# Scores of two attentions as three products of split queries and keys, and raw weights in pieces

## The chip, the cores and the metric

The kernel runs on one core of one Trainium2 chip. The metric is the device time of one execution in microseconds (us), lower is better; three runs of the kernel before gave 2064.75, 2060.04 and 2063.96, and their median, 2063.96, is the time before.

## The reference

Two transformer-like blocks on 256 tokens of width 1024, each two layers deep, all in float32. What matters here is where scores are formed:

```python
# first block, per layer: three branches on h = rms_norm(x)
y_a = mamba2_branch(...)                 # chunked state-space scan
y_b = sliding_window_branch(...)         # "banded": 16 heads of 64, 4 key heads, window 128, rope, sinks
#   scores = einsum('bnqkgd,bnskd->bnkgqs', qb, kb) * HEAD_DIM ** -0.5
y_c = forgetting_attention_branch(...)   # 16 heads, causal, decay by cumulated gates, no rope
x = x + sum(sigmoid(gate_i) * (y_i @ w_proj_i)) @ w_out

# second block, per layer: tokens x and a context of 256 tokens, 8 heads, 2 key heads
q, k = apply_rope(q), apply_rope(k)      # the tokens' own, not the context's
s_lat = einsum('bnqhgd,bnkhd->bhgnqk', qb, kb) * scale     # blocks of 128, neighbours within 128
s_ctx = einsum('bnqhgd,bchd->bhgnqc', qb, kc) * scale      # 256 context keys
o = softmax([s_lat, s_ctx, sink]) @ [v, vc]
# in layer 0 the context attends to itself as well; then pool, fourier, merge, conv_ffn
```

## The kernel before

The width lies on the 128 partitions, 8 chunks of it, with the 256 tokens along the free axis (512 in the second block's first layer, where tokens and context run together).

**Dense products.** Every weight matrix is multiplied in three products of split operands (`mm3`): high part by high part, high by low, low by high. The parts are of type fp32r, a form of float32 that TensorE takes in one pass. A unit of weights is a [128, 2048] tile. `fetch` loads it raw as one DMA of 1 MB on SyncE's queue (tile `wr`), then in four pieces of 512 ScalarE copies the high part (`wh`, recorded at line L98) and VectorE, or GpSimd for one of the pieces, subtracts to get the low part (`wl`, L101). The three tiles each have 3 buffers, so the loads run about two units ahead. Only the first units, for which a callback `between` is given, come in four DMAs.

**Scores.** The attentions multiply plain float32: `qk` (L234) forms the scores of two heads, which stand on partitions 0 to 63 and 64 to 127, for the banded and the forgetting branch; the inner function `score` of `attention` does so in the second block, with 512 keys in two halves of 256. Queries and keys are turned by `rope`: four small DMAs swap halves into a second tile, GpSimd and VectorE multiply, VectorE adds (tiles `f` from a ring of 13, later 10 buffers; `swk` for the banded keys, `kv` for the second block's keys and values).

**Order.** The order of TensorE's instructions is the order in which the code issues them: a running count of rows gives a `tick` each 3072 rows (`spent`), and a tick advances the waiting tasks (rope, weights) and the attention jobs, each in three steps (scores; transposes of the probabilities; values). So the attention's small pieces stand at fixed places among the dense products. The other engines' instructions are put in order by a scheduler at build time. Pools with a fixed number of buffers decide who waits for whom.

All TensorE work is recorded at L92 (matmul) and L95 (transpose), ScalarE's at L98, VectorE's at L101 and L104, since helpers issue it: the groups are told apart by their tiles. `pd` is the PSUM tile of dense products, `ps` of scores, `pt` of transposes, `po` of values.

Of the kernel before, what the change touches and what calls it, by code (L numbers as in the profile page):

```python
# [6 lines left out]
F32 = mybir.dt.float32  # L7
F32R = mybir.dt.float32r
# [3 lines left out]
ALU = mybir.AluOpType  # L12
# [33 lines left out]
class Kern:  # L46
    def __init__(self, ctx, tc, A, out, dbg=None):
        self.tc, self.nc, self.A, self.out = tc, tc.nc, A, out
        self.dbg = dbg or {}
        nc = tc.nc  # L50
        self.V, self.S, self.P, self.T = nc.vector, nc.scalar, nc.gpsimd, nc.tensor
        p = lambda name, bufs, **kw: ctx.enter_context(tc.tile_pool(name=name, bufs=bufs, **kw))
        self.cst_p = p("cst", 1)
        self.w_p = p("w", 3)
        self.wl_p = p("wlo", 3)
        self.x_p = p("x", 1)
        self.m_p = p("wm", 2)
        self.r_p = p("r", 3)
        self.sm_p = p("sm", 2)
        self.dram_p = p("dram", 1, space=bass.MemoryType.DRAM)  # L60
        self.ps_d = p("psd", 3, space=PSUM)
        self.ps_s = p("pss", 2, space=PSUM)
        self.ps_t = p("pst", 2, space=PSUM)
        self.ps_o = p("pso", 1, space=PSUM)
        self.t = self.rows = 0
        self.on_pool = (1024,)
        self.tasks = []
        self.jobs = []
        self.waiting = []
        self.cur = self.nxt = None  # L70
# [44 lines left out]
    def fetch(self, between=None, on_pool=None):  # L115
        ap, kt, ncol = self.queue.pop(0)
        n = kt * ncol
        on_pool = self.on_pool if on_pool is None else on_pool
        raw = self.w_p.tile([128, 2048], F32, name="wr", tag="wr")
        hi = self.w_p.tile([128, 2048], F32R, name="wh", tag="wh")  # L120
        lo = self.wl_p.tile([128, 2048], F32R, name="wl", tag="wl")
        if between is None:
            self.nc.sync.dma_start(raw[:, :n], ap)
        step = 512
        for o in range(0, n, step):
            s = slice(o, o + step)
            if between is not None:
                between(o // step)
                self.nc.sync.dma_start(raw[:, s], ap[:, s])
            self.act(hi[:, s], raw[:, s])  # L130
            self.tt(lo[:, s], raw[:, s], hi[:, s].bitcast(F32), ALU.subtract, self.P if o in on_pool else None)
        v = lambda t: t[:, :n].rearrange("p (k c) -> p k c", k=kt)
        self.ready.append((v(hi), v(lo)))

# [99 lines left out]
    def qk(self, pss, cuts, q, k):  # L234

        for a, b, c, d in cuts:
            for i, ps in enumerate(pss):
                p = slice(64 * i, 64 * i + 64)
                self.mm(ps[:, a:b], q[p, 128 * (a > 0):128 * (a > 0) + 128], k[p, c:d], True, True)

    def masked(self, out, ps, mask, least, init=3e38):

# [267 lines left out]
def b1_layer(K, l, x, yr, sums, cw, wdt, first_sums=None):  # L510
# [210 lines left out]
    for i in range(4):  # L721
# [26 lines left out]
        def score(pair, pss, q=q, kk=kk, i=i):  # L748
            K.qk(pss, ((0, 128, 0, 128), (128, 384, 0, 256)), q[:, pair, :], kk[:, pair, :])
# [22 lines left out]
            K.tt(m, m, th, ALU.add, K.P)  # L772


    def rope(t):
        s = K.f2((128, 2, 256))
        for a in range(4):
            b = a ^ 1
            nc.scalar.dma_start(s[32 * a:32 * a + 32], t[32 * b:32 * b + 32])

        def task():
            yield 2
            K.tt(s, s, K.bc(K.rope[:, 1, :], 2), ALU.mult, K.P)
            K.tt(t, t, K.bc(K.rope[:, 0, :], 2), ALU.mult)
            yield 1
            K.tt(t, t, s, ALU.add)

        turned = K.spawn(task())
        K.step(turned)
        return turned  # L790

    ps = K.dense(K.unit(), H, (0, 1))
    kk = K.k_p.tile([128, 2, 256], F32, name="swk", tag="k0")
    K.act(kk, ps)
    kturned = rope(kk)
    ps = K.dense_tok(K.unit(), H)
    v = K.k_p.tile([128, 2, 256], F32, name="swv", tag="k1")
    K.act(v, ps)
    yb = K.r_p.tile([128, 2, NK, 256], F32R, name="yb", tag="r16")
    nsk = K.small([128, 16], "nsk")  # L800
# [1 line left out]
    for i in range(4):  # L802
        g0 = 2 * (i // 2)
        ps = K.dense(K.unit(), H, (0, 1))
        q = K.f2((128, 2, 256))
        K.act(q, ps, scale=-0.125)
        turned = rope(q)
        zs = gate_z(K.dense(K.unit(), H, (0, 1)))

        def score(pair, pss, q=q, i=i):  # L810
            K.qk(pss, ((0, 128, 0, 128), (128, 384, 0, 256)), q[:, pair, :], kk[:, i // 2, :])

        def fix(pair, i=i):
            s = slice(4 * i + 2 * pair, 4 * i + 2 * pair + 2)
            return (nsk[:, s],
                    vec("sink", 16 * l, 16)[:, s].unsqueeze(2).to_broadcast([128, 2, 2]))

        js = attn4(score, lambda j, t, g0=g0: v[:, t, 64 * (g0 + j % 2):64 * (g0 + j % 2) + 64],
                   (K.msk("u"), K.msk("le", 2)), fix, gated(yb, zs, 2 * i), 2, (turned, kturned))
        jb += js  # L820
        gate_proj(2, yc, i, jc, True)
# [196 lines left out]
def b2_layer(K, l, x, hin, last, after):  # L1018
# [25 lines left out]
    cs64 = c2[:, 3072:3328]  # L1044
    poolw = c2[:, 3328 + 256 * l:3328 + 256 * l + 256].rearrange("p (c d) -> p c d", c=2)

    def rope(t):

        sw = K.f2((128, 256))
        for q in range(4):  # L1050
            b = q ^ 1
            nc.scalar.dma_start(sw[32 * q:32 * q + 32], t[32 * b:32 * b + 32])
        def task():
            yield 2
            K.tt(sw, sw, K.rope2[:, 1, :], ALU.mult, K.P)
            K.tt(t, t, K.rope2[:, 0, :], ALU.mult)
            yield 1
            K.tt(t, t, sw, ALU.add)

        turned = K.spawn(task())  # L1060
        K.step(turned)
        return turned


    kt = K.kv[:, 0:512]
    v = K.kv[:, 512:1024].rearrange("p (t c) -> p t c", t=4)
    yp = r16((128, 2, 4, 512), "yp2", K.rx_p)
    ya = r16((128, 2, 4, 512), "ya2")
# [51 lines left out]

    def keys(s, Hs):
        ps = K.dense(wkv, Hs, (0, 1))
        K.act(kt[:, tok(s)], ps[:, 0, :])
        if s == 0:
            turned_k.append(rope(kt[:, 0:256]))
        vtasks.append(K.spawn(values_task(s, ps[:, 1, :])))

    def pools(s, Hs):
# [95 lines left out]
    def attention(pair, q, turned):  # L1224
        sh, js = {}, []

        def done(o):
            split(ya[:, 0, pair, 0:W], ya[:, 1, pair, 0:W], o)

        for qb in range(2):  # L1230
            def score(pss, qb=qb):
                for a in range(2):
                    for i, ps in enumerate(pss):
                        p = slice(64 * i, 64 * i + 64)
                        K.mm(ps[:, 256 * a:256 * a + 256], q[p, 128 * qb:128 * qb + 128],
                             kt[p, 256 * a:256 * a + 256], True, True)

            js.append(attn_pair(sh, pair, 128 * qb, score, 1, K.msk("lt" if qb else "zero", 4), lambda b, i: v[:, b, 64 * i:64 * i + 64],
                                done if last and qb else None))
        if not last:  # L1240
            def score(pss):
                for qb in range(2):
                    for i, ps in enumerate(pss):
                        p = slice(64 * i, 64 * i + 64)
                        K.mm(ps[:, 256 * qb:256 * qb + 256], q[p, 256 + 128 * qb:384 + 128 * qb], kt[p, 256:512],
                             True, True)

            js.append(attn_pair(sh, pair, 256, score, 2, None, lambda b, i: v[:, 2 + b % 2, 64 * i:64 * i + 64], done))
        return K.enqueue(js, 1, (turned, *keyed))

    ja = []
    for i in range(2):
        w = K.unit(1 if last and i == 0 else 2)
        for job in jobs:
            q = K.f2((128, len(job), W))
            K.act(q, K.dense(w, H, job), scale=-0.125)
            if last and i == 0:
                project(1, (keys,))
            keyed = turned_k + vtasks
            for ci, c in enumerate(job):  # L1260
                turned = rope(q[:, ci, 0:256])
                ja += attention(2 * i + c, q[:, ci, :], turned)

    K.finish(*ptasks)
    merged = K.big_p.tile([128, NK, W], F32, name="merged2", tag="m")
# [303 lines left out]
def program(tc, A, out, dbg=None):  # L1569
    with ExitStack() as ctx:  # L1570
# [14 lines left out]
        with ExitStack() as c1:  # L1585
            p = lambda name, bufs, **kw: c1.enter_context(tc.tile_pool(name=name, bufs=bufs, **kw))
            K.big_p, K.sm1_p, K.k_p = p("big1", 1), p("sm1", 1), p("k1", 1)
            K.f_p = p("f1", 13)
            K.ones = K.cst_p.tile([128, 128], F32, name="ones")
            V.memset(K.ones, 1.0)  # L1590
            warm = K.small([128, 1], "warm")
# [50 lines left out]
            def between(js):  # L1642
                b1_raw(K, 1, x1, yr, js)
                if js.start == 4:
                    wdt.extend(b1_wdt(K, 1))
# [45 lines left out]
        with ExitStack() as c2:  # L1691
# [2 lines left out]
            K.f_p = p("f2", 10)  # L1694
            kv = K.m_p.tile([128, 2048], F32, name="kv", tag="wm")
            K.kv = kv[:, 0:1024]
            K.rope2 = kv[:, 1024:1536].rearrange("p (c n) -> p c n", c=2)
            nc.sync.dma_start(K.rope2, A["rope2"])

# [248 lines left out]
```

## Time and profile before

| | us |
|---|---|
| median of three runs | 2063.96 |
| the profiled execution | 2062.68 |
| its span on the core | 2060.9 |
| TensorE (PE) busy | 2029.2 (98%) |
| VectorE (DVE) busy | 1464.4 (71%) |
| ScalarE (ACT) busy | 991.1 (48%) |
| GpSimd (POOL) busy | 506.2 (25%) |
| mean granted TensorE clock | 0.994 |

PE's matmuls are recorded with overlapping ends, so its busy time counts stretches without a gap: what one product costs is read from the distance between two starts. An instruction that shows an idle time in brackets waited for the instruction behind the arrow. Busy times of the other engines count only where PE waits for them.

### The profile page before, as it was taken

Reading aid. Unit: us, or ns where it says so; the run is one execution under the profiler, and the core shown is the slowest. Engines: PE = TensorE matmul, PEld = TensorE weight load, DVE = VectorE, ACT = ScalarE, POOL = GpSimd, SP = SyncE. Lnnn points to the kernel's source line nnn. Section 1 sums busy time; section 2 is a strip of 40 time slices with the busy share of each in tenths; the row PEclk is TensorE's granted clock in tenths of the full one; section 3 lists DMA queues with packets and bytes.
Section 4 is the critical chain, followed back from the end, with each engine's and each line's share of the span. In section 5 each row is a group of like instructions: output and inputs, shape, how many; then the busy total and the mean of one; then the engine's idle time right before and its main releaser. Section 6 shows DMA issues by size and latency. Waiting matters only on the chain.

```text
span 2060.9 us, 37605 instructions
## 1 busy us (share of the span) xinstructions
PE 2029.2 (98%) x14768; PEld 1839.0 (89%) x14768; DVE 1464.4 (71%) x2835; ACT 991.1 (48%) x2112; POOL 506.2 (25%) x393
## 2 busy tenths in 40 slices
PE   8999999999999999999999999999999999999998
PEld 7898999999898999999877888888888899999997
DVE  7777788976777788978466454865564576879984
ACT  6455555545455555555344333542332354556553
POOL 3232222324333123343100212111111121232222
PEclk9999999999999999999999999999999999999999
DMA  7765656665765656654111232232222233454552
GB/s 272 292 214 191 219 207 248 222 246 203 259 208 195 233 202 243 231 191 162 59 57 57 87 123 102 83 102 94 91 103 92 92 128 118 144 195 164 182 192 77
DMA packets 66304, 339.08 MB, mean 165 GB/s; under 512 B 7760, under 2 KB 22096, under 8 KB 29776
## 3 DMA queue, kind: packets, MB, share of 16 engines
q1 hardware_dynamic: 62000, 332.22, 45.7%
q10 hardware_dynamic: 4128, 4.46, 0.8%
q8 instruction: 116, 1.90, 0.4%
q14 instruction: 60, 0.49, 0.1%
HBM read 331.28 MB, written 1.44 MB: 161 GB/s over the span
## 4 chain that ended last, share of the span: by engine, by line
PE 92%; DVE 5%; issue 1%; ACT 1%; DMA 1%; SPq 0%; POOL 0%; DVEq 0%; POOLq 0%; ACTq 0%
PE pd L92 81%; PE ps L92 4%; PE po L92 3%; PE pt L92 2%; PE pt L95 2%; DVE wl L101 2%; DVE f L104 1%; DVE f L101 1%; ACT wh L98 0%; DMA wm<-in_wm_dram 0%; DVE h L104 0%; DMA x<-in_x_dram 0%; DVE f L984 0%; DVE hl L101 0%; ACT f L98 0%
## 5 line engine op out<-in xcount | busy, mean ns | idle before, releaser
L101 DVE TENSOR_TENSOR wl<-wr,wh 128x512 fp32r<-128x512 f32 x751 | 687.9, 934 | 244.7 <-ACT wh L98 243.1
L98 ACT ACTIVATE wh<-wr 128x512 fp32r<-128x512 f32 x992 | 561.2, 621 | 470.1 <-PE pd L92 262.1
L101 POOL TENSOR_TENSOR wl<-wr,wh 128x512 fp32r<-128x512 f32 x241 | 349.9, 1452 | 1238.9 <-ACT wh L98 1103.0
L92 PE MATMUL pd<-h,wh 128*128 128x256 f32 x2688 | 498.7, 286 | 2.4 <-ACT wh L98 1.4
L92 PEld LDWEIGHTS pd<-h,wh 128*128 128x128 f32 x2688 | 417.5, 191 | 26.4 <-issue 17.6
L92 PE MATMUL pd<-h,wl 128*128 128x256 f32 x1344 | 380.0, 283 | 0.7 <-DVE wl L101 0.7
L92 PE MATMUL pd<-hh,wh 128*128 128x512 f32 (+1 forms) x992 | 347.6, 350 | 1.5 <-ACT hh L98 1.5
L92 PE MATMUL pd<-hl,wh 128*128 128x512 f32 (+1 forms) x992 | 341.4, 344 | 3.7 <-DVE hl L101 3.7
L92 PE MATMUL pd<-hh,wl 128*128 128x512 f32 (+1 forms) x992 | 340.4, 343 | 0.0
L92 PEld LDWEIGHTS pd<-h,wl 128*128 128x128 f32 x1344 | 257.2, 191 | 1.2 <-DVE wl L101 0.9
L92 PEld LDWEIGHTS pd<-hh,wh 128*128 128x128 f32 x992 | 189.9, 191 | 30.4 <-issue 7.5
L92 PEld LDWEIGHTS pd<-hl,wh 128*128 128x128 f32 x992 | 190.1, 192 | 25.5 <-DVE hl L101 4.7
L92 PEld LDWEIGHTS pd<-hh,wl 128*128 128x128 f32 x992 | 190.0, 192 | 21.6
L92 PE MATMUL pd<-act,wh 128*128 128x256 f32 (+1 forms) x688 | 160.2, 327 | 0.0
L104 DVE SCALAR_TENSOR_TENSOR f<-pd,cw,f 128x255 f32<-128x255 f32 (+3 forms) x272 | 151.0, 555 | 11.0 <-ACT f L98 8.6
L92 PEld LDWEIGHTS pd<-act,wh 128*128 128x128 f32 x688 | 116.2, 190 | 11.1 <-DVE act L101 0.2
L92 PE MATMUL pd<-hf,wh 128*128 128x256 f32 x640 | 115.2, 283 | 0.0
L92 PE MATMUL pd<-mg,wh 128*128 128x256 f32 (+1 forms) x576 | 113.0, 296 | 0.1
L92 PE MATMUL pd<-act,wl 128*128 128x256 f32 (+1 forms) x344 | 112.2, 326 | 0.0
L98 ACT ACTIVATE f<-f,mn 128x128 f32<-128x128 f32 (+2 forms) x160 | 79.8, 500 | 46.8 <-DVE mn L243 46.6
L98 ACT ACTIVATE f<-pd,cw 128x256 f32<-128x256 f32 (+1 forms) x120 | 66.8, 557 | 69.6 <-DVE f L104 62.7
L92 PEld LDWEIGHTS pd<-hf,wh 128*128 128x128 f32 x640 | 99.8, 192 | 0.0
(257 smaller groups left out, 3216.5 us busy)
## 6 DMA issues: line engine op xcount, KB each, us to landing
wr<-in_w_dram SPq DMA_DIRECT2D x233, 1024.0 KB, 4.9
wm<-in_wm_dram SPq DMA_DIRECT2D x48, 1024.0 KB, 6.9
f<-far SPq DMA_DIRECT2D x32, 192.0 KB, 5.1
f<-far SPq DMA_DIRECT2D x24, 256.0 KB, 6.0
wr<-in_wd_dram SPq DMA_DIRECT2D x8, 768.0 KB, 4.2
wr<-in_wa_dram SPq DMA_DIRECT2D x8, 512.0 KB, 3.5
c<-in_c_dram SPq DMA_DIRECT2D x2, 1920.0 KB, 7.8
f<-f ACTq DMA_DIRECT2D x32, 64.0 KB, 2.0
```

Of the source, the lines that this page charges most:

```text
L92: self.T.matmul(out, l, r, start=start, stop=stop)
L95: self.T.transpose(out, in_, self.ident[0:k, 0:k])
L98: self.S.activation(out, in_, f, **kw)
L101: (eng or self.V).tensor_tensor(out, a, b, op=op)
L104: self.V.scalar_tensor_tensor(out, a, s, b, op0=op0, op1=op1)
```

## The change

Three things are changed. (1) The raw weights get a pool of their own, ten pieces of [128, 512], and every unit comes in four DMAs of 256 KB, each issued just ahead of its copy. (2) In the banded branch and in the second block, queries and keys are split after the rope into a high and a low part of type fp32r, one copy on ScalarE and one subtraction on VectorE each; where no rope is applied (the context), the parts are taken from PSUM. (3) The scores are then three products of these parts. In the second block the 512 keys stand in one product. The forgetting branch keeps its float32 scores. The ring of `f` grows from 13 to 15 buffers in the first block, with the room that the smaller raw tiles leave.

```diff
+        self.wr_p = p("wraw", 10)
...
     def fetch(self, between=None, on_pool=None):
-        raw = self.w_p.tile([128, 2048], F32, name="wr", tag="wr")
...
-        if between is None:
-            self.nc.sync.dma_start(raw[:, :n], ap)
...
+            raw = self.wr_p.tile([128, 512], F32, name="wr", tag="wr")
+            self.nc.sync.dma_start(raw, ap[:, s])
+            self.act(hi[:, s], raw)
+            self.tt(lo[:, s], raw, hi[:, s].bitcast(F32), ALU.subtract, self.P if o in on_pool else None)
...
+    def qk3(self, pss, cuts, q, k):
+        (qh, ql), (kh, kl) = q, k
+        for a, b, c, d in cuts:
+            t = slice(128 * (a > 0), 128 * (a > 0) + 128)
+            for n, (x, y) in enumerate(((qh, kh), (qh, kl), (ql, kh))):
+                for i, ps in enumerate(pss):
+                    p = slice(64 * i, 64 * i + 64)
+                    self.mm(ps[:, a:b], x[p, t], y[p, c:d], n == 0, n == 2)
...
     # first block, rope
             K.tt(t, t, s, ALU.add)
+            K.act(parts[0], t)
+            K.tt(parts[1], t, parts[0].bitcast(F32), ALU.subtract)
...
-            K.qk(pss, ((0, 128, 0, 128), (128, 384, 0, 256)), q[:, pair, :], kk[:, i // 2, :])
+            K.qk3(pss, ((0, 128, 0, 128), (128, 384, 0, 256)), [t[:, pair, :] for t in q],
+                 [t[:, i // 2, :] for t in kk])
...
     # second block, rope
             K.tt(t, t, sw, ALU.add)
+            split(*parts, t)
...
+        def scores(pss, cuts):
+            for t0, c0, ks in cuts:
+                for n, (a, b) in enumerate(((0, 0), (0, 1), (1, 0))):
+                    for i, ps in enumerate(pss):
+                        p = slice(64 * i, 64 * i + 64)
+                        K.mm(ps[:, c0:c0 + ks.stop - ks.start], q[a][p, t0:t0 + 128], kt[b][p, ks], n == 0, n == 2)
...
-                for a in range(2):
-                    for i, ps in enumerate(pss):
-                        p = slice(64 * i, 64 * i + 64)
-                        K.mm(ps[:, 256 * a:256 * a + 256], q[p, 128 * qb:128 * qb + 128],
-                             kt[p, 256 * a:256 * a + 256], True, True)
+                scores(pss, [(128 * qb, 0, slice(0, 512))])
...
+                scores(pss, [(256 + 128 * qb, 256 * qb, slice(256, 512)) for qb in range(2)])
...
-            q = K.f2((128, len(job), W))
-            K.act(q, K.dense(w, H, job), scale=-0.125)
+            qs = [K.f2((128, len(job), W), F32R) for _ in range(2)]
+            q = K.f2((128, len(job), 256))
+            ps = K.dense(w, H, job)
+            K.act(q, ps[:, :, 0:256], scale=-0.125)
+            if not last:
+                K.act(qs[0][:, :, 256:512], ps[:, :, 256:512], scale=-0.125)
+                K.stt(qs[1][:, :, 256:512], ps[:, :, 256:512], -0.125, qs[0][:, :, 256:512].bitcast(F32),
+                      ALU.mult, ALU.subtract)
...
-            K.f_p = p("f1", 13)
+            K.f_p = p("f1", 15)
...
+            K.kt = K.big_p.tile([128, 2, 512], F32R, name="kt")
```

TensorE, at the first banded score of layer 0: `ps` are the two heads' score tiles, `swk` the keys, `f` the queries. The first piece is before, the second now.

```order
L92 MATMUL po<-f_2084,f_1220 64x128
L92 MATMUL ps<-swk,f_1908 128x128 x2
L92 MATMUL ps<-swk,f_1908 128x256 x2
L92 MATMUL pd<-yc,wh 128x256 x2
L92 MATMUL pd<-yc,wl 128x256
```

```order
L93 MATMUL po<-f_2230,f_1304 64x128
L93 MATMUL ps<-swk_1827,f_2040 128x128 x2
L93 MATMUL ps<-swk_1828,f_2040 128x128 x2
L93 MATMUL ps<-swk_1827,f_2041 128x128 x2
L93 MATMUL ps<-swk_1827,f_2040 128x256 x2
L93 MATMUL ps<-swk_1828,f_2040 128x256 x2
L93 MATMUL ps<-swk_1827,f_2041 128x256 x2
L93 MATMUL pd<-yc,wh 128x256 x2
L93 MATMUL pd<-yc,wl 128x256
```

The place is the same, four matmuls have become twelve, and nothing beside them has moved; it is so at all 16 banded scores.

In the second block four products of 256 columns have become six of 512, at the same place, in 16 scores; 4 scores of the context have twice three pairs of 256.

VectorE, at the third banded score of layer 0 (the first of the second group of queries): `f<-f,rope` and the `f<-f,f` after `yb` are the rope's product and sum, `wl` are low parts of weights.

```order
L101 TENSOR_TENSOR f_2307<-f_2307,rope 128x512
L101 TENSOR_TENSOR wl<-wr,wh 128x512 x2
L104 SCALAR_TENSOR_TENSOR f_2398<-po,f_2011 128x512
L101 TENSOR_TENSOR wl<-wr,wh 128x512
L104 SCALAR_TENSOR_TENSOR f_2402<-f_2402,pd 128x512
L101 TENSOR_TENSOR yb<-f_2398,yb 128x512
L101 TENSOR_TENSOR f_2307<-f_2307,f_2309 128x512
L101 TENSOR_TENSOR wl<-wr,wh 128x512
```

```order
L102 TENSOR_TENSOR f_2481<-f_2481,rope 128x512
L102 TENSOR_TENSOR wl<-wr,wh 128x512 x2
L105 SCALAR_TENSOR_TENSOR f_2580<-po,f_2149 128x512
L102 TENSOR_TENSOR wl<-wr,wh 128x512
L105 SCALAR_TENSOR_TENSOR f_2584<-f_2584,pd 128x512
L102 TENSOR_TENSOR yb<-f_2580,yb 128x512
L102 TENSOR_TENSOR f_2481<-f_2481,f_2485 128x512
L102 TENSOR_TENSOR f_2484<-f_2481,f_2483 128x512
L102 TENSOR_TENSOR wl<-wr,wh 128x512 x2
```

Up to the sum nothing has moved; the low part of the queries, `f_2484`, comes right behind it, and reads the high part `f_2483` that ScalarE copies from the sum.

ScalarE, in the second block's layer 1, around its first score: `f<-pd 128x512` are the second group's queries, the DMAs are their rope's swaps, and `f_19016` (now) are the high parts of the first group's queries, which the first score reads.

```order
L98 ACTIVATE wh<-wr 128x512
L98 ACTIVATE f_17785<-pd 128x512
L98 ACTIVATE wh<-wr 128x512
L1052 DMA f_17849<-f_17785 32x256 x4
L1052 DMA f_17854<-f_17785 32x256 x4
L98 ACTIVATE wh<-wr 128x512 x2
```

```order
L99 ACTIVATE wh<-wr 128x512
L99 ACTIVATE f_19196<-pd 128x512
L99 ACTIVATE wh<-wr 128x512
L1065 DMA f_19260<-f_19196 32x256 x4
L1065 DMA f_19265<-f_19196 32x256 x4
L99 ACTIVATE wh<-wr 128x512 x2
L99 ACTIVATE f_19016<-f_19018 128x256 x2
```

What stood there stands there still, and the two copies have come behind it.

VectorE, in layer 0's forgetting branch: the `COPY` takes transposed probabilities of a head out of PSUM for the values' products (`po`).

```order
L683 TENSOR_SCALAR f_998<-f_998,den 128x256
L101 TENSOR_TENSOR wl<-wr,wh 128x512 x6
L693 COPY f_1191<-pt 128x384
L104 SCALAR_TENSOR_TENSOR f_1255<-po,f_540 128x512
```

```order
L691 TENSOR_SCALAR f_1070<-f_1070,den 128x256
L102 TENSOR_TENSOR wl<-wr,wh 128x512 x3
L701 COPY f_1275<-pt 128x384
L102 TENSOR_TENSOR wl<-wr,wh 128x512 x3
```

The copy has moved ahead of three low parts; on ScalarE the other head's copy has moved ahead of four high parts in the same way. On GpSimd, in layer 1, where the forgetting branch ends and the banded keys are turned, one low part that stood just ahead of the last mask and the keys' rope product now stands one mask earlier. On SyncE each unit's one load has become four, with the loads of other tensors among them.

## Rows read from the trace of the kernel before

**Rows 1.** The page: the chain that ended last, by engine.

```profile
PE 92%; DVE 5%; issue 1%; ACT 1%; DMA 1%; SPq 0%; POOL 0%; DVEq 0%; POOLq 0%; ACTq 0%
```

**Rows 2.** Waits of PE: engine, line, releaser: total us, times, longest.

```profile
PE ps L92 <- ACT wh L98: 5.8, 1, 5.8
...
PE po L92 <- DVE f L693: 1.9, 1, 1.9
...
PE pt L95 <- DVE f L683: 1.3, 1, 1.3
```

**Rows 3.** Timeline of PE at one second-block score: start, us, instruction, count so far.

```profile
1788.57 0.70 PE L92 MATMUL ps<-kv,f 64*128 64x256 f32 x4
1788.89 0.60 PE L92 MATMUL ps<-kv,f 64*128 64x256 f32 x4
...
1789.32 0.38 PE L92 MATMUL ps<-kv,f 64*128 64x256 f32 x2
1789.63 0.39 PE L92 MATMUL pd<-hh,wh 128*128 128x256 f32 x1
```

**Rows 4.** Timeline of PE at one banded score.

```profile
170.94 0.93 PE L92 MATMUL ps<-swk,f 64*128 64x128 f32 x8
171.80 0.39 PE L92 MATMUL pd<-yc,wh 128*128 128x256 f32 x1
```

**Rows 5.** Timeline of PE: first and last of 15 products of 512 columns, of 22 of 256.

```profile
1028.52 0.39 PE L92 MATMUL pd<-hh,wh 128*128 128x512 f32 x1
...
1031.72 0.40 PE L92 MATMUL pd<-hh,wl 128*128 128x512 f32 x1
...
1789.98 0.28 PE L92 MATMUL pd<-hh,wl 128*128 128x256 f32 x1
...
1792.49 0.28 PE L92 MATMUL pd<-hh,wl 128*128 128x256 f32 x1
```

**Rows 6.** By form: low and high parts of `h`, busy us, mean ns, idle before.

```profile
L101 DVE TENSOR_TENSOR hl<-f,hh 128x512 fp32r<-128x512 f32 x24 | 17.0, 724 | 0.4 <-ACT hh L98 0.3
...
L98 ACT ACTIVATE hh<-f 128x512 fp32r<-128x512 f32 x24 | 14.4, 621 | 4.2 <-DVE f L984 4.2
```

**Rows 7.** Timeline: the rope's sum, ScalarE, and the banded score, first and last.

```profile
198.09 0.68 DVE L101 TENSOR_TENSOR f<-f,f 128x512 f32<-128x512 f32 x1
...
199.05 0.93 PE L92 MATMUL ps<-swk,f 64*128 64x128 f32 x8
...
199.09 1.15 ACT L98 ACTIVATE wh<-wr 128x512 fp32r<-128x512 f32 x2 [2.05 <-PE pd L92]
...
730.33 0.68 DVE L101 TENSOR_TENSOR f<-f,f 128x512 f32<-128x512 f32 x1
...
731.45 0.93 PE L92 MATMUL ps<-swk,f 64*128 64x128 f32 x8
```

**Rows 8.** Timeline of ACT (ACTq: its DMA issues) and PE, second block, layer 1.

```profile
1714.45 0.58 ACT L98 ACTIVATE f<-pd 128x512 f32<-128x512 f32 x1
...
1715.06 5.01 ACTq L1052 DMA_DIRECT2D f<-f  x8
1720.12 1.15 ACT L98 ACTIVATE wh<-wr 128x512 fp32r<-128x512 f32 x2 [4.57 <-DMA f<-f]
...
1716.98 1.13 PE L92 MATMUL ps<-kv,f 64*128 64x256 f32 x8
```

**Rows 9.** Timeline, DVE and PE, at the forgetting branch's values in layer 0.

```profile
99.80 0.55 DVE L693 COPY f<-pt 128x384 f32<-128x384 f32 x1
...
100.40 0.87 PE L92 MATMUL po<-f,f 128*64 128x256 f32 x8 [1.89 <-DVE f L693]
```

**Rows 10.** Timeline of DVE at the sum of the banded keys' rope, layer 1.

```profile
620.41 0.69 DVE L101 TENSOR_TENSOR swk<-swk,f 128x512 f32<-128x512 f32 x1 [1.82 <-POOL f L101]
```

**Rows 11.** Busy by stretch: PE, PEld, DVE, ACT, POOL, PEclk, DMA share, GB/s.

```profile
0.00:12.00 12.00, 6.18 (x34) 5.95 (x35) 5.96 (x13) 7.27 (x14) 0.20 (x4) 1.00 0.79 249
12.00:30.00 18.00, 17.10 (x143) 16.69 (x142) 14.93 (x44) 9.52 (x21) 5.93 (x4) 1.00 1.02 415
```

More of the change, by code (lines that the diff above doesn't have):

```diff
@@ L118, in fetch @@
         on_pool = self.on_pool if on_pool is None else on_pool
-        raw = self.w_p.tile([128, 2048], F32, name="wr", tag="wr")
         hi = self.w_p.tile([128, 2048], F32R, name="wh", tag="wh")
         lo = self.wl_p.tile([128, 2048], F32R, name="wl", tag="wl")
-        if between is None:
-            self.nc.sync.dma_start(raw[:, :n], ap)
-        step = 512
-        for o in range(0, n, step):
-            s = slice(o, o + step)
-            if between is not None:
[L128 to L131, printed above, removed]
+        for o in range(0, n, 512):
+            s = slice(o, o + 512)
+            if between is not None:
+                between(o // 512)
+            raw = self.wr_p.tile([128, 512], F32, name="wr", tag="wr")
+            self.nc.sync.dma_start(raw, ap[:, s])
+            self.act(hi[:, s], raw)
+            self.tt(lo[:, s], raw, hi[:, s].bitcast(F32), ALU.subtract, self.P if o in on_pool else None)
         v = lambda t: t[:, :n].rearrange("p (k c) -> p k c", k=kt)
@@ L772, in gate_proj, with rope @@
             K.tt(m, m, th, ALU.add, K.P)
-    def rope(t):
+    def rope(t, parts):
         s = K.f2((128, 2, 256))
@@ L792, in b1_layer @@
     ps = K.dense(K.unit(), H, (0, 1))
-    kk = K.k_p.tile([128, 2, 256], F32, name="swk", tag="k0")
-    K.act(kk, ps)
-    kturned = rope(kk)
+    kk = [K.k_p.tile([128, 2, 256], F32R, name="swk%d" % n, tag="k%d" % n) for n in range(2)]
+    kf = K.f2((128, 2, 256))
+    K.act(kf, ps)
+    kturned = rope(kf, kk)
     ps = K.dense_tok(K.unit(), H)
-    v = K.k_p.tile([128, 2, 256], F32, name="swv", tag="k1")
+    v = K.k_p.tile([128, 2, 256], F32, name="swv", tag="k2")
     K.act(v, ps)
@@ L806, in b1_layer, with score @@
         K.act(q, ps, scale=-0.125)
-        turned = rope(q)
+        qs = [K.f2((128, 2, 256), F32R) for _ in range(2)]
+        turned = rope(q, qs)
         zs = gate_z(K.dense(K.unit(), H, (0, 1)))
-        def score(pair, pss, q=q, i=i):
-            K.qk(pss, ((0, 128, 0, 128), (128, 384, 0, 256)), q[:, pair, :], kk[:, i // 2, :])
+        def score(pair, pss, q=qs, i=i):
+            K.qk3(pss, ((0, 128, 0, 128), (128, 384, 0, 256)), [t[:, pair, :] for t in q],
+                 [t[:, i // 2, :] for t in kk])
         def fix(pair, i=i):
@@ L1045, in b2_layer, with rope @@
     poolw = c2[:, 3328 + 256 * l:3328 + 256 * l + 256].rearrange("p (c d) -> p c d", c=2)
-    def rope(t):
+    def rope(t, parts):
         sw = K.f2((128, 256))
@@ L1062, in rope @@
         return turned
-    kt = K.kv[:, 0:512]
+    kt = K.kt[:, 0, :], K.kt[:, 1, :]
     v = K.kv[:, 512:1024].rearrange("p (t c) -> p t c", t=4)
@@ L1122, in keys @@
         ps = K.dense(wkv, Hs, (0, 1))
-        K.act(kt[:, tok(s)], ps[:, 0, :])
+        ks = [t[:, tok(s)] for t in kt]
         if s == 0:
-            turned_k.append(rope(kt[:, 0:256]))
+            k = K.f2((128, 256))
+            K.act(k, ps[:, 0, :])
+            turned_k.append(rope(k, ks))
+        else:
+            split(*ks, ps[:, 0, :])
         vtasks.append(K.spawn(values_task(s, ps[:, 1, :])))
@@ L1241, in score @@
             def score(pss):
[L1242 to L1246, printed above, removed]
+                scores(pss, [(256 + 128 * qb, 256 * qb, slice(256, 512)) for qb in range(2)])
             js.append(attn_pair(sh, pair, 256, score, 2, None, lambda b, i: v[:, 2 + b % 2, 64 * i:64 * i + 64], done))
@@ L1260, in b2_layer @@
             for ci, c in enumerate(job):
-                turned = rope(q[:, ci, 0:256])
-                ja += attention(2 * i + c, q[:, ci, :], turned)
+                turned = rope(q[:, ci, :], [t[:, ci, 0:256] for t in qs])
+                ja += attention(2 * i + c, [t[:, ci, :] for t in qs], turned)
     K.finish(*ptasks)
```

## The prediction

> **What bounds the kernel now.** I read the chain that ended last first: 92% of it is TensorE [rows 1], so an edit counts only through TensorE's own time or through a wait of TensorE. Its waits come next; the longest single one is 5.8 us at the start, and two that matter here are 1.9 and 1.3 us [rows 2]. Then I read TensorE's timeline where scores stand, and VectorE's and ScalarE's timelines ahead of those scores, since the split of queries and keys is put between the rope and the score. The order of TensorE's work is the same in both kernels but for the scores themselves.
>
> **The scores, second block.** One score took 1789.63 - 1788.57 = 1.06 us from its first start to the next dense product, and two of its steps took 1789.32 - 1788.89 = 0.43, so 0.215 each [rows 3]. The row of x4 (two heads by two steps) is 0.60 long where x2 is 0.38: the two heads, on different halves of the rows, run side by side. Four steps are 0.86; 0.20 is the edge on both sides, which stays. An fp32r product of 512 columns has a pitch of (1031.72 - 1028.52)/14 = 0.229, one of 256 columns (1792.49 - 1789.98)/21 = 0.120 [rows 5]. Now 3 x 0.229 = 0.686 stand in place of 0.86: -0.174, times 16 scores, -2.8 us. The four context scores go from 0.86 to 6 x 0.120 = 0.72: -0.6 us. Together -3.4.
>
> **The scores, banded.** One took 171.80 - 170.94 = 0.86 us [rows 4]; less the same edge, 0.66 for two steps of 128 and two of 256 columns, so 0.66 - 0.43 = 0.23 for the two of 128. The new one has three products of 256 (0.36) and three of 128. No fp32r product of 128 columns occurs in this trace. From below its price is by columns alone a quarter of the 512 one, 0.057; from above it is what a float32 product of 128 columns costs, 0.23. Between them lies the row of 256 columns, 0.120; as one step of a float32 product of 128 columns takes 0.115, I take 0.120. Then the score is 0.72 in place of 0.66, times 16: +1.1 us (ends: -2.0 and +6.2).
>
> The Trainium skill ("FP8 and Floating Point Precision", TensorE Precision Notes) counts true FP32 as four passes of products of halves; three products would then be three quarters of the price at any width, 0.66 x 0.75 = 0.50, and the banded scores would give back 16 x 0.16 = 2.6 us. The trace does not agree for 256 columns, where the three cost 0.36 against 0.43, five sixths. Against it speaks the skill's "TensorE: Matmul & The Clock Gate" (LDWEIGHTS), by which loading weights takes time by their columns, P/1.2 ns, an estimate of 107 ns for 128 whatever streams through: by that rule the narrow product saves nothing, and the sum would be that of 0.120 or a little less.
>
> **The split, banded.** It adds a copy on ScalarE, 0.62, and a subtraction on VectorE, 0.72 [rows 6], behind the rope's sum, five times per layer. Where the sum is early that hides beside dense products, and it costs nothing. It is not early: at the third score the sum starts at 198.09 and ends at 198.77, with no idle time of VectorE in its row, and the score starts at 199.05, a margin of 0.28; the last such pair has 730.33 + 0.68 = 731.01 against 731.45, 0.44 [rows 7]. Of the eight query groups five look like this, the last three of layer 0 and the last two of layer 1; I take the mean of these two margins, 0.36. The third product needs the low part, which comes 0.62 + 0.72 = 1.34 after the sum, with hand-overs of about 0.05 each (the copy of the forgetting branch ends at 100.35, the matmul that waits for it starts at 100.40 [rows 9]) 1.5. It is due 0.36 + 0.1 + 2 x 0.12 = 0.70 after the sum (the 0.1 being the half of the edge that lies ahead). So TensorE waits 0.8 us, five times: +4.0 (ends: 0, if the sum comes 0.8 earlier, and 5 x 1.2 = 6, if the weights' load of the late part shows too). ScalarE is free there, it stands idle for 2.05 us until 199.09 [rows 7]. Behind the subtraction VectorE has low parts of weights, which wait for ScalarE and so for TensorE anyway; nothing else is late for it.
>
> **The split, second block.** In layer 0 the copies stand behind single waits and I cost them at nothing; dense products hide them. In layer 1 they do not: the high parts of the first group's queries stand on ScalarE behind the swaps of the second group's rope. These are eight DMA issues, and an issue holds the engine: from 1715.06 on they took 5.01 us, and the two weight copies behind them started only at 1720.12, after 4.57 us of idle time, and took 1.15 [rows 8]. The high part comes then at 1721.27 + 0.4 (an estimate from the 0.62 of twice the columns) = 1721.7. The score that reads it started at 1716.98 [rows 8]. TensorE is to wait 4.7 us there: +4.7 (ends: 3.5, if the weight copies take no time ahead of it, and 5.6, if the low part of VectorE is late too). All later scores of the layer find their parts ready, as the second group's copies have a whole group's scores ahead of them.
>
> **What the order gives back.** TensorE waited 1.89 us at 100.40 for a copy of VectorE that ended at 100.35 [rows 9]. It stood behind six low parts of weights and now stands behind three, with the other head's copy moved in the same way on ScalarE; the wait goes: -1.9. In layer 1 the sum of the keys' rope waited 1.82 us for GpSimd [rows 10], and behind it the forgetting branch's normalisation made TensorE wait 1.3 [rows 2]. GpSimd's low part now comes one mask earlier, into what was idle time: -1.3 (ends: -1.3 and 0). What is late next in both places is nothing that these views show.
>
> **The raw weights in pieces.** In steady state a piece of the ring is free when its own subtraction is done, not a whole unit's; TensorE hardly waits for weights there. I cost it at nothing. At the start it is different: until 12 us loads come in rows of 2 KB and move 249 GB/s at a share of 0.79, so 315 at full share; from 12 to 30 us mostly in rows of 8 KB, and move 415 at a share of 1.02, saturated [rows 11]. If the rows' length is the reason, the same data take up to 18 x 415/315 - 18 = 5.7 us longer, of which TensorE, busy for 17.10 of the 18 us, would feel some; pieces on the other hand let the copies start a piece earlier, against a first wait of 5.8 [rows 2]. I take 0, from -1 to +3.
>
> **Sum.** -3.4 + 1.1 + 4.0 + 4.7 - 1.9 - 1.3 + 0 = +3.2 us on the profiled execution's 2062.68, so 2065.9. That execution lies 1.3 below the median of the runs, 2063.96; the same step from there gives 2067.2.
>
> **Rivals.**
> - *Narrow fp32r products cost what float32 ones cost* (0.23 in place of 0.120). For it: the only rows with 128 columns are float32. Against it: nothing in the trace. It adds 16 x 3 x 0.11 = 5.3: 2072.5, slower. It decides from about 0.14 a product on.
> - *The scores' waits do not come, but the gains do* (the sums of the rope move ahead, the issues are short): without 4.0 and 4.7 the time is 2058.5, faster. Against it: the order of VectorE up to the sum and of ScalarE up to the copies is unchanged.
> - *Only the long wait in layer 1 fails to come*, since ScalarE's issues end earlier: 2062.5.
> - *Narrow products cost by columns alone*: 16 x 3 x 0.063 = 3.0 less, 2064.2. For it: the step from 512 to 256 columns nearly halves the price. Against it: 256 columns cost a little more than half, and float32's narrow step, 0.115, more than half of its wide one, 0.215. By the Trainium skill's rule of four passes, above, the time would come near this one too.
> - *Heads do not run side by side in fp32r.* Then a score is 6 x 0.229 against 0.86 (+0.51, 16 times), the context's +0.58 four times, a banded one 12 x 0.12 - 0.66 (+0.78, 16 times): 23 us over before in place of 2.3 under it, 2092. Against it: the halves of the rows are what separates the heads in rows 3, and that stays.
>
> **Chances.** My sum 0.50 (its own range 2064 to 2071), narrow products dear 0.25, no long wait 0.10, no waits at all 0.07, by columns 0.05, heads one after the other 0.03. 0.2% of this time, about what a measurement tells from no change, is 4.1 us: faster means below 2059.8, slower above 2068.1. Faster: 0.07 x 0.6 + 0.10 x 0.1 + a little = 0.06. Slower: 0.50 x 0.4 + 0.25 x 0.9 + 0.03 = 0.46. The rest, 0.48, is the same. The range 2060 to 2073 leaves out the last rival, some of the first and most of the second, under 0.2 together.
>
> **What the profile after would show.** Pitches: key products of 512 columns at 0.229, of 128 at 0.12 (0.23 if the first rival holds), each score's two heads starting together. Waits of TensorE: five of about 0.8 on the banded scores for a VectorE `f`, one of 4 to 5 us at the second block's layer 1 for a ScalarE `f`, and those at 100 and 622 us gone. If the waits for scores sum to under 4 us, or the start differs by over 3 us, my sum was wrong in that term; a time below 2060 would make the waits wrong, one above 2073 the price of a product.

## The result and the profile after

The change makes the kernel slower: 2083.53 us median of six runs (2078.91 to 2084.77) against 2063.72 of the kernel before, also six runs, a ratio of 1.0094 with a 95% interval of 1.0080 to 1.0108. I had forecast 2067.2, within 2060 to 2073. The profiled execution took 2083.52 us, span 2081.7, 20.8 us over the one shown before.

The waits of TensorE in the kernel after (total us, times, longest), those that answer to [rows 2]:

```profile
PE ps L93 <- ACT f L99: 12.1, 6, 4.5
...
PE ps L93 <- DVE f L102: 2.9, 7, 1.1
PE po L93 <- DVE f L701: 1.8, 2, 1.2
...
PE pt L96 <- DVE f L691: 1.6, 1, 1.6
```

The first two rows are new: scores that wait for the high parts (ScalarE's copies, `ACT f`) and the low parts (VectorE's, `DVE f`), 15.0 us together. The wait that my -1.3 was to take away, for the forgetting branch in layer 1, stands at 1.6 in place of 1.3; the other (1.9 at 100 us) is gone, since the two left in `po` are at other places.

Where the time goes can be read by matching the two kernels' TensorE instructions, which but for the scores stand in one order, and taking the difference of their start times (after less before). It is -2.6 us at 146 us of the kernel before, +9.0 at 287, behind layer 0's banded branch (11.6 lost there), +7.4 at 588, +7.7 at 628, +15.2 at 749, behind layer 1's (7.5 lost), +15.5 at 970, +14.8 at 1151, still so at 1715, +22.4 at 1735 (7.6 lost at the first score of the second block's layer 1), +21.2 at the end.

**The long wait.** Timeline of ScalarE and TensorE there, after, which answers to [rows 8]:

```profile
1729.79 5.03 ACTq L1065 DMA_DIRECT2D f<-f  x8
1734.87 1.15 ACT L99 ACTIVATE wh<-wr 128x512 fp32r<-128x512 f32 x2 [4.59 <-DMA f<-f]
1735.93 0.71 ACT L99 ACTIVATE f<-f 128x256 fp32r<-128x256 f32 x2
...
1736.38 1.22 PE L93 MATMUL ps<-kt,f 64*128 64x512 f32 x4 [4.55 <-ACT f L99]
1738.71 0.79 PE L93 MATMUL ps<-kt,f 64*128 64x512 f32 x2 [1.11 <-DVE f L102]
```

Eight issues hold ScalarE for 5.03 us, two weight copies follow, then the high part, and TensorE waits 4.55 for it (I had said 4.7) and another 1.11 for the low part. What I had not counted is the row after: the granted clock. By stretch (columns as in [rows 11]; the clock is the number ahead of the DMA share):

```profile
1731.00:1734.00 3.00, 0.83 (x8) 0.59 (x6) 0.43 (x2) 0.00 (x0) 0.00 (x0) 1.00 0.70 229
1734.00:1737.00 3.00, 0.62 (x4) 0.50 (x4) 1.78 (x2) 1.76 (x4) 2.34 (x3) 0.72 0.12 34
1737.00:1740.00 3.00, 1.89 (x8) 0.86 (x5) 2.90 (x7) 0.00 (x0) 0.77 (x1) 0.50 0.45 147
1740.00:1743.00 3.00, 3.00 (x20) 3.00 (x19) 2.02 (x8) 1.61 (x5) 0.00 (x0) 0.65 0.08 27
```

TensorE stood still for most of 1732 to 1736; then it ran at 0.50, its lower level of 1.2 GHz, and came back to 2.4 GHz some 6 us later. Of the 7.6 us lost 5.7 are the two waits, about 2 the clock.

**A banded score.** Layer 0 has eight, two for each of four groups of queries. This is the first of the fourth group, after: GpSimd, VectorE, ScalarE and TensorE in the order of the chain:

```profile
258.36 1.81 POOL L102 TENSOR_TENSOR f<-f,rope 128x512 f32<-128x512 f32 x1 [2.14 <-DMA f<-f]
...
258.32 0.69 DVE L102 TENSOR_TENSOR f<-f,rope 128x512 f32<-128x512 f32 x1 [1.56 <-DMA f<-f]
...
264.74 0.68 DVE L102 TENSOR_TENSOR f<-f,f 128x512 f32<-128x512 f32 x1
...
265.46 0.63 ACT L99 ACTIVATE f<-f 128x512 fp32r<-128x512 f32 x1 [1.77 <-DVE f L102]
...
263.57 0.28 PE L93 MATMUL pd<-h,wl 128*128 128x256 f32 x1
266.14 0.44 PE L93 MATMUL ps<-swk,f 64*128 64x128 f32 x4 [2.29 <-ACT f L99]
266.87 0.73 PE L93 MATMUL ps<-swk,f 64*128 64x128 f32 x8 [0.29 <-DVE f L102]
```

Before, the same product, sum and score:

```profile
251.74 1.77 DVE L101 TENSOR_TENSOR f<-f,rope 128x512 f32<-128x512 f32 x1
...
258.14 0.68 DVE L101 TENSOR_TENSOR f<-f,f 128x512 f32<-128x512 f32 x1
...
259.18 0.93 PE L92 MATMUL ps<-swk,f 64*128 64x128 f32 x8
```

After, the rope's sum ends at 265.42; the score was due about 0.2 behind the product of 263.57. So the sum itself, the same instruction as before, is 1.6 late, and the split adds the rest. Before, it ended 0.36 ahead of its score. From the product to the sum VectorE takes 6.4 us in both kernels; the sum is late because the rope's products wait for the swap DMAs (1.56 on VectorE, 2.14 on GpSimd), where before VectorE's did not wait. The swaps take longer, by the pages' DMA rows, before and after (the last number is the median time from issue to landing; x40 after because the keys' eight swaps, before a row of their own with 2.1, are among them):

```profile
f<-f ACTq DMA_DIRECT2D x32, 64.0 KB, 2.0
```

```profile
wr<-in_w_dram SPq DMA_DIRECT2D x936, 256.0 KB, 3.4
...
f<-f ACTq DMA_DIRECT2D x40, 64.0 KB, 3.9
```

The Trainium skill ("DMA: Bandwidth & Descriptors", Queues, rings and completion order) says that each DMA engine takes turns between the queues that have work for it, a packet at a time. The trace fits that: during these swaps (251 to 257 us) the engines move four pieces of weights as well, while in the kernel before (246.5 to 252.5) they had little else to do once the tail of one unit was in. The landing times of single swaps go further than the medians. In the kernel before, 36 of the first block's 40 swaps land in 1.9 to 2.1 us. The other four take 3.4, 3.5, 5.3 and 5.7 us, and they are those that were issued behind a load of `far` or of `in_wm_dram` or within 0.3 us ahead of one; the last two (SyncE's timeline, then the DMA view from 629.70 to 630.95 us):

```profile
629.95 1.19 SPq L458 DMA_DIRECT2D wm<-in_wm_dram  x2
...
f<-f ACTq DMA_DIRECT2D x2, 64.0 KB, 5.5
```

In the kernel after, every one of the 40 has a load close by: 28 were issued at most 2.2 us behind one and take 2.9 to 5.9 us; the other 12 have one only behind them, and nine of these take 1.9 to 2.1. So swaps are late beside loads of 1 MB too; the pieces put a load beside every group of them. No run moved the loads away, so this is read from landing times and not shown by experiment.

The last late sum, that of the fourth group in layer 1, is late in another way. VectorE's product there does not wait for the swaps. Their four issues hold ScalarE for 3.45 us in place of 2.45, the weight copies behind them come a us later, and so does the low part that VectorE makes ahead of the product. ScalarE before and after, then VectorE after:

```profile
718.93 2.45 ACTq L779 DMA_DIRECT2D f<-f  x4
...
732.29 3.45 ACTq L787 DMA_DIRECT2D f<-f  x4
...
736.97 1.41 DVE L102 TENSOR_TENSOR wl<-wr,wh 128x512 fp32r<-128x512 f32 x1 [2.08 <-ACT wh L99]
```

Behind the wait at 266 us too the clock falls, for about 3.4 us, and comes back:

```profile
265.00:267.00 2.00, 0.57 (x6) 0.43 (x8) 1.30 (x3) 1.54 (x3) 0.00 (x0) 1.00 0.55 177
267.00:269.00 2.00, 2.00 (x15) 1.86 (x16) 2.00 (x9) 1.85 (x6) 1.22 (x1) 0.64 0.27 80
269.00:271.00 2.00, 2.00 (x11) 2.00 (x11) 1.34 (x6) 1.99 (x9) 0.16 (x1) 0.51 0.83 255
271.00:273.00 2.00, 2.00 (x19) 2.00 (x19) 1.05 (x5) 0.00 (x0) 0.00 (x0) 1.00 0.59 199
```

The matched starts slip another 1.5 us in these stretches (from 7.5 to 9.0), and so they do behind the waits of the third banded group of layer 0 and of the third of layer 1.

### The profile page after: what moved, and what is told of

It is laid out like the page before. It is cut to its first block, busy times and chain, and to the rows that moved or that the text cites. A ratio compares the mean times of both kernels' runs of the same rounds, so it can differ in the third digit from the quotient of the medians.

```text
span 2081.7 us, 39564 instructions
## 1 busy us (share of the span) xinstructions
PE 2035.8 (98%) x14816; PEld 1846.7 (89%) x14816; DVE 1469.6 (71%) x2861; ACT 1002.1 (48%) x2136; POOL 508.3 (24%) x393
## 4 chain that ended last, share of the span: by engine, by line
PE 63%; DVE 4%; DMA 1%; ACT 1%; issue 1%; ACTq 0%; POOL 0%; DVEq 0%; POOLq 0%
PE pd L93 57%; PE ps L93 2%; PE pt L93 2%; PE po L93 1%; PE pt L96 1%; DVE wl L102 1%; DMA f<-f 1%; DVE f L102 1%; ACT f L99 0%; DVE hl L102 0%; ACT wh L99 0%; DVE f L105 0%; DVE f L997 0%; ACTq L787 0%; DMA wr<-in_w_dram 0%
## 5 line engine op out<-in xcount | busy, mean ns | idle before, releaser
L99 ACT ACTIVATE f<-f 128x512 f32<-128x512 f32 (+4 forms) x100 | 58.3, 591 | 90.2 <-DVE f L105 44.4
```

Of the source, the lines that this page charges most:

```text
L99: self.S.activation(out, in_, f, **kw)
```

## Experiments

Every run has its ratio to the kernel before, timed on the same chip, with a 95% interval. Differences between experiments of different rounds hold to about 1 us, since the kernel before had medians from 2062.6 to 2063.7 us in them.

**1. Pieces alone.** The new `fetch`, ring of ten and 15 buffers of `f`; scores and ropes as before.

> Raw weights in ten pieces and the ring of f at 15, scores in float32 as before. Theory A (the pieces' loads run beside the rope's swap DMAs, which land in 3.9 us in place of 2.0, so the rope's sum is late by itself): swaps land in over 3 us, TensorE waits for the sum (DVE f) at the second, third and fourth banded groups of layer 0 and the last two of layer 1, about 1.5 us twice and 0.5 us twice; less the two waits that the new order takes away, the time is 2063 to 2067. Rival B (the pieces are innocent, the split alone is to blame): swaps land in 2 us, no such waits, 2060 to 2062.

Measured 2060.9, ratio 0.9995 (0.9985 to 1.0004): no difference. The swaps' DMA row of its page:

```profile
f<-f ACTq DMA_DIRECT2D x32, 64.0 KB, 3.5
```

and the one wait of TensorE for a score (total us, times, longest):

```profile
PE ps L93 <- DVE f L102: 0.9, 1, 0.9
```

Both theories half missed: the swaps do land in 3.5, as A said, but only one score waits, 0.9, and the time is in B's range. The unsplit sum has just enough margin. So the pieces alone are not the cost; they eat the margin that the split then needs.

**2. Banded split alone, with whole units.**

```diff
# fetch, ring and second block as before; in the banded branch
-        turned = rope(q)
+        qs = [K.f2((128, 2, 256), F32R) for _ in range(2)]
+        turned = rope(q, qs)
...
+            K.qk3(...)
```

> Units of 1 MB as before, only the banded queries and keys split, three products. Theory A: swaps land in 2 us, five waits of TensorE of about 1 us each (copy and subtraction behind a sum that is in time), no fall of the clock: 2068 to 2071. Rival B: the waits are those of the full change, about 9 us in all with one or two over 2 us, and the granted clock falls behind them: 2075 to 2080.

Measured 2077.81, ratio 1.0074 (1.0057 to 1.0090), in B's range, but not by B's waits. Its waits of TensorE for scores are 4.2 us, near what A gave, and its swaps land in 2.1 (DMA row). The waits, the first of them not for a score:

```profile
PE pt L95 <- DVE f L693: 4.2, 1, 4.2
...
PE ps L92 <- ACT f L98: 2.8, 4, 1.4
...
PE ps L92 <- DVE f L101: 1.4, 5, 0.3
```

The swaps' DMA row:

```profile
f<-f ACTq DMA_DIRECT2D x40, 64.0 KB, 2.1
```

Of the rest, a wait of 4.2 at 627 us is the largest part: this kernel's own order puts the keys' rope, with its wait for the swaps, ahead of the forgetting branch's normalisation on VectorE. The clock falls to 0.50 behind it, and 5.3 us are lost there.

```profile
627.21 0.69 DVE L101 TENSOR_TENSOR f<-f,rope 128x512 f32<-128x512 f32 x1 [4.91 <-DMA f<-f]
```

Those swaps were issued beside loads of `far` and of a unit of 1 MB and took up to 7.1 us: the median of 2.1 hides 16 of 40 that take over 2.5. Eleven of the 16 have no load close by, so loads are not the only thing that delays a swap; what delayed these is open. The profiled execution was also the longest of the four (2082.88); about 2.9 us of it went to a fall of the clock at 1688 us, behind a pause that the kernel before has too (at 1671 us, clock 1.00). A kernel with part of a change has an order of its own, and its time is not the part's price.

**3. Pieces and the second block's split.** Banded scores in float32.

> Pieces as in the change, only the second block's queries and keys split. Both theories: one wait of 4.5 us at the second block's layer 1 with half the clock behind it, 7.5 us together, and about 1.7 us given back by shorter scores: 5 to 6 us over the kernel with pieces alone. Theory A for the sum: 2069 to 2073; rival B: 2066 to 2068.

Measured 2067.3, ratio 1.0027 (1.0016 to 1.0038): 6.4 over the pieces alone, a little more than the 5 to 6 of both, and in B's range. The long wait is here as well, so it is the second block's own:

```profile
PE ps L93 <- ACT f L99: 4.5, 1, 4.5
```

**4. Halves of a unit in place of quarters.**

```diff
-            raw = self.wr_p.tile([128, 512], F32, name="wr", tag="wr")    # 10 buffers
-            self.nc.sync.dma_start(raw, ap[:, s])
+            half = self.wr_p.tile([128, 1024], F32, name="wr", tag="wr")  # 5 buffers
+            self.nc.sync.dma_start(half, ap[:, o:o + 1024])
```

> The whole change, but the ring of raw weights is five halves of [128, 1024], loaded by one DMA of 512 KB each, the same room. Theory A, if what matters is that a load starts as soon as a part of a unit is used up: swaps land between 2.5 and 3.5 us, waits for scores 8 to 13 us in place of 15, 2075 to 2082. If what matters is the row length alone (2 KB against 4 and 8): swaps land in about 2.5 us. Rival B: unchanged, 2082 to 2085.

Measured 2094.1, ratio 1.0152 (1.0137 to 1.0167), worse than the change and above both ranges. Swaps 4.2, waits for high parts 16.9:

```profile
PE ps L93 <- ACT f L99: 16.9, 7, 4.5
```

The swaps' DMA row:

```profile
f<-f ACTq DMA_DIRECT2D x40, 64.0 KB, 4.2
```

Rows of 4 KB in place of 2 do not make the swaps faster, so short rows are not what makes them late.

**5. A ring of six pieces in place of ten.**

```diff
-        self.wr_p = p("wraw", 10)
+        self.wr_p = p("wraw", 6)
```

> The whole change with a ring of six pieces in place of ten. If pieces in flight beside the swaps make the sum late: swaps land in 2 to 3.2 us in place of 3.9, the banded waits shrink by a third or more, 2070 to 2080, unless weights come late. If the number in flight does not matter: 2081 to 2085.

Measured 2083.82, ratio 1.0100 (1.0085 to 1.0116), as the change; swaps 3.7. The number of pieces in flight is not it either. That the swaps are late wherever weights come in parts is shown by the medians (3.4 to 4.2 in every kernel with parts, 2.0 and 2.1 in all with units); which property of the parts does it no experiment shows. The landing times above speak for the moment of the loads' issue: a unit's load starts when all four of its predecessor's pieces are used, a piece's with every copy and subtraction, and the swaps are issued among those.

**6. The banded sum moved.** The sum and the split in the same tick as the rope's products. TensorE's order is the same as the change's, row for row, here and in the next two.

```diff
             K.tt(t, t, K.bc(K.rope[:, 0, :], 2), ALU.mult)
-            yield 1
             K.tt(t, t, s, ALU.add)
```

> The whole change, but the banded rope's sum, and with it the split, is issued in the same tick as the rope's products; TensorE's order stays. Theory (the banded waits come from a sum that stands just ahead of its score and is moved further back by late swaps and by the split): the sum ends 3 us or more ahead of the score, the banded waits of 9 us and the falls of the granted clock behind them go, 2064 to 2068. Rival (VectorE has too much to do there, wherever the sum stands): the waits stay over 5 us, 2076 to 2084.

Measured 2068.49, ratio 1.0024 (1.0015 to 1.0033): 15.0 us less than the change, just over the range that I gave. Of the waits for scores only the long one is left, with swaps at 3.9 as in the change:

```profile
PE ps L93 <- ACT f L99: 4.6, 1, 4.6
...
PE ps L93 <- DVE f L102: 0.9, 1, 0.9
```

The swaps' DMA row:

```profile
f<-f ACTq DMA_DIRECT2D x40, 64.0 KB, 3.9
```

The sum now ends 1.5 us or more ahead of the score in every group (I had expected 3). The split costs VectorE and ScalarE as much as in the change, so it was not their load that made the kernel slow but the place of the sum.

**7. The last layer's sum moved in the second block.**

```diff
             K.tt(t, t, K.rope2[:, 0, :], ALU.mult)
-            yield 1
+            if not last:
+                yield 1
             K.tt(t, t, sw, ALU.add)
```

> The whole change, but in the second block's last layer the rope's sum is issued in the same tick as its products, which puts the high parts of the first group's queries ahead of the eight swaps of the second group on ScalarE; TensorE's order stays. Theory (ScalarE's DMA issues hold the high part back): the wait of 4.5 us and the half clock behind it go, 7 to 8 us less than the full change, 2075 to 2077. Rival (the second group's load and swaps hold it in another way): under 3 us less.

Measured 2075.41, ratio 1.0066 (1.0051 to 1.0082): 8.1 less than the change. The high parts of the first group now stand ahead of the eight swaps on ScalarE, and the long wait and the fall of the clock behind it are gone:

```profile
1725.32 0.42 ACT L99 ACTIVATE f<-f 128x256 fp32r<-128x256 f32 x1 [1.42 <-DVE f L102]
...
1727.42 5.03 ACTq L1065 DMA_DIRECT2D f<-f  x8
```

**8. Both moves.**

> Both moves. If the waits explain the slowdown and the scores' price is the small gain that the sum had: 2056 to 2061. If the split costs something else: over 2064.

Measured 2059.75, ratio 0.9984 (0.9976 to 0.9993). TensorE waits for no split score any more; the same banded score as above, VectorE's sum and low part, then TensorE:

```profile
256.27 1.78 DVE L102 TENSOR_TENSOR f<-f,f 128x512 f32<-128x512 f32 x1
...
259.17 0.68 DVE L102 TENSOR_TENSOR f<-f,f 128x512 fp32r<-128x512 f32 x1
...
259.73 0.95 PE L93 MATMUL ps<-swk,f 64*128 64x128 f32 x12
260.62 0.51 PE L93 MATMUL pd<-yc,wh 128*128 128x256 f32 x2
```

With 23.8 us less than the change it has taken back all that the change lost, and a little more: the score's own price, 260.62 - 259.73 = 0.89 against 0.86 [rows 4], and in the second block

```profile
1785.77 0.96 PE L93 MATMUL ps<-kt,f 64*128 64x512 f32 x6
1786.65 0.38 PE L93 MATMUL pd<-hh,wh 128*128 128x256 f32 x1
```

0.88 against 1.06 [rows 3].

**9. Pieces, second block's split and its moved sum, banded in float32.**

> Pieces, and only the second block's split, with the sum of its last layer moved as above; banded scores in float32. It has the shorter scores of the second block without the banded split: 2 to 4 us under the kernel with pieces alone (2060.9), 2057 to 2060, faster than before if any version is.

Measured 2060.59, ratio 0.9984 (0.9976 to 0.9993), no better than 8 and just over the range that I gave: one banded sum is late again here, and TensorE waits 1.5 us for it.

**10. The same with the banded sum moved.**

> Pieces, the second block's split with its last layer's sum moved, the banded rope's sum moved, and banded scores in float32. Theory: it keeps the shorter scores of the second block (3 us), has no banded split (0.5 us of scores and its copies less than the kernel with both moves) and no late sum: 2056 to 2059, the fastest. Rival: the moved sum does something of its own, over 2061.

Measured 2056.78, ratio 0.9973 (0.9964 to 0.9983): in the range that I gave, the lowest of all, faster than the kernel before. Its interval overlaps those of 8 and 9, so that it beats them is not shown.

**11. Banded split with units and the sum moved.**

> Units of 1 MB, only the banded split, with the banded rope's sum moved ahead. Theory: no wait of TensorE for a banded score, 2062 to 2066 but for the wait at 630 us that the order of the kernel without the move had (4 us and the clock), which the moved sum may leave, then up to 2070. Rival (the split itself is dear): over 2074.

Measured 2072.78, ratio 1.0052 (1.0036 to 1.0068), over the range that I gave. No banded score waits, which is what it was for; between the first and the last banded score of layer 0 the matched starts slip by 0.8 us in place of 3.9 in experiment 2, in layer 1 by 0.2 in place of 4.4. But the wait at 630 us is still there (3.7), another of 2.9 follows it, and 8.2 us are lost around them:

```profile
PE pt L95 <- DVE f L693: 3.7, 1, 3.7
```

## Why the prediction was wrong, point by point

- **Scores, second block: right.** I had -2.8 and -0.6. Matched over all 16 and 4: 1.064 to 0.893 and 1.064 to 0.907 us, -2.7 and -0.6 (experiment 8).
- **Scores, banded: right in kind, smaller.** 0.856 to 0.884 over 16, +0.45 for my +1.1 (0.06 times 16 is 1.0; I had added it up wrongly by 0.1). Narrow fp32r products start 0.11 apart (my 0.120), the two heads' products at the same time. The rivals of dear narrow products, of heads one after the other and of price by columns alone are out.
- **"So TensorE waits 0.8 us, five times: +4.0": this step failed.** It took the rope's sum to end where it ended before, about 0.36 ahead of the score. All five scores that I named waited, and of the others only one, 0.3 us. But at the third score the sum ended 0.1 behind the due time, and the wait was 0.76 + 0.29 = 1.05 us; at the others it was late by 1.5 and 1.6 us at the last two groups of layer 0 and by 0.5 and 0.6 at those of layer 1. At three of these four VectorE's product waited for swaps (1.8, 1.6 and 0.8 us), which land in 3.9 in place of 2.0; at the last one the issues of the swaps held ScalarE longer. The waits for banded scores came to 9.3, 9.0 of them at the five. With whole units they came to 4.2 (experiment 2), so the price of the split alone was right.
- **"In steady state [...] I cost it at nothing": this step failed with it.** I looked for weights that come late and found rightly that none would; I did not ask what else uses the DMA engines at that moment. Alone the pieces cost nothing (experiment 1, 0.9 us of waits for banded scores); with a sum that had 0.1 to 0.4 us to spare and 1.4 us of split put behind it they did.
- **Waits priced at their length: failed.** Four of them were followed by some 3.4 us (banded) or 6 us (second block) at the lower clock, which cost 1.5 us each in the banded branch and 2 in the second block, 6.6 together, and no term of the sum held that.
- **The long wait: right.** 4.55 for my 4.7, and gone when the order on ScalarE is turned round; the low part's further 1.11 I had as an upper end.
- **What the order gives back: half right.** The 1.9 us at 100 us went. The 1.3 in layer 1 did not: GpSimd's masks there waited 3.04 us for the load of `far`, so that the earlier low part freed nothing:

```profile
626.28 1.31 POOL L102 TENSOR_TENSOR f<-f,mask 128x256 f32<-128x256 f32 x2 [3.04 <-DMA f<-far]
```

- **The start: right.** The difference was +0.3 us at 66 us.

The sum of what was measured: -2.9 scores, -1.9 the copy, +9.3 banded waits, +5.7 the long one, +6.6 clock, 16.8; of the 20.8 of the two profiled executions 4 are spread over small places, the largest a wait for `po` of about 1.2 us ahead of layer 1's first banded score and the slip of 1.4 ahead of layer 0's. These I did not test one by one.

## What to carry to other kernels

Before work is put behind an instruction, read how far ahead of its reader that instruction ends and what it waits for; here 0.1 to 0.4 us were left, and small DMAs that land late beside loads of weights stood at the chain's head. When a change puts more loads on the DMA engines, ask which small transfers run at that moment. Issuing the small chain a tick earlier left TensorE's order as it was and was worth 24 us, while the arithmetic saved 3. Price a wait of TensorE with the clock behind it, not by its length.

## What the runs showed of the hardware

- The clock: waits of 2.1 + 0.3, 2.3 + 0.3 and 1.1 + 0.3 us were each followed by about 3.4 us at 1.2 GHz. Another of 1.2 + 0.3 us (at 745 us, kernel after) was followed by none; the granted clock there stayed at 1.00. So length alone does not decide it at this size.

```profile
746.00:748.00 2.00, 1.61 (x16) 1.33 (x17) 1.91 (x4) 2.00 (x5) 0.25 (x1) 1.00 0.13 48
```

- Small DMAs from ScalarE's queue, 64 KB, land in 2.0 us (median) with weights in loads of 1 MB and in 3.4 to 4.2 with loads of 256 or 512 KB, at nearly the same mean rate of all DMAs (165 and 163 GB/s, before and after). Single ones that were issued beside a load took 3.4 to 5.7 us in the kernel before and 2.9 to 5.9 after.
- Four issues of such DMAs held ScalarE for 2.45 us at one place of the kernel before and for 3.45 at the same place after; eight, of 32 KB each, held it for 5.03.
- fp32r products of 128 columns with 64 rows start 0.11 us apart, as one float32 step of 128 columns does (0.11), and those of 256 columns 0.12: half the columns save next to nothing.
